# A hybrid HGRN2 and gated DeltaNet layer on one core: TensorE's order written down in halves of projections

## The chip, the cores and the metric

The kernel runs on one core of a Trainium2 chip, as one launch. The time is that of the device, in microseconds (us), for the whole program. "PE" is TensorE (matrix products), "DVE" VectorE, "ACT" ScalarE, "POOL" GpSimd, "SP" the engine whose queue issues nearly all DMAs here. PEld is TensorE's weight load, which runs beside its matmuls.

## The reference

One layer of a backbone over 2048 latent tokens and 256 context tokens, width 1024. A normalised and modulated input `h` goes through one projection of 9248 columns. Eight heads of kind A (HGRN2, a gated linear recurrence) and eight of kind B (gated DeltaNet, with a 3x3 depthwise convolution on q, k and v) scan the tokens forward and backward in chunks; both scans of the latents start from the state that the context leaves. The head outputs are normalised, gated, put through one output projection, added to the input and normalised again.

```python
def project(h, w_in, conv_w, lb, a_log, dt_bias, rows):
    y = jnp.einsum("bld,dn->bln", h, w_in)
    a_q, a_f_fwd, a_f_bwd, a_i, a_z, b_q, b_k, b_v, b_z, b_a, b_b = split_columns(y)
    ...
    qkv = jax.nn.silu(grid_conv(jnp.concatenate([b_q, b_k, b_v], axis=-1), conv_w, rows))

# group A, one chunk (hgrn2_scan)
        s_new = d_last[..., 0, :, None] * s + jnp.einsum("bhsk,bhsv->bhkv", k_dec, v_i)
        scores = jnp.einsum("bhtk,bhsk,bhtsk->bhts", q_i, k_i, dec)
        o = jnp.einsum("bhtk,bhkv->bhtv", q_dec, s) + jnp.einsum("bhts,bhsv->bhtv", scores, v_i)

# group B, one chunk (gdn_scan); u0 and w come from a triangular solve with the chunk's keys
        v_new = u0_i - jnp.einsum("bhck,bhkv->bhcv", w_i, s)
        s_new = d_last[..., None, None] * s + jnp.einsum("bhck,bhcv->bhkv", k_dec, v_new)
        o = jnp.einsum("bhtk,bhkv->bhtv", q_dec, s) + jnp.einsum("bhts,bhsv->bhtv", p_i, v_new)

# group_out, then the residual and the last norm
    y_a = jax.nn.silu(z_a) * head_norm(o_a, na_w)
    y_b = jax.nn.silu(z_b) * head_norm(o_b, nb_w)
    return jnp.concatenate([y_a, y_b], axis=-1) @ w_out
```

## The kernel before, in words

Tokens are worked in 9 groups of 256 (the context and eight of latents), each of two blocks of 128. Projections run in float16 with every operand split into a high and a low part: one step over 128 input channels is three matmuls (high by high, low by high, high by low), so a projection of one column block for one group is 8 x 3 = 24 matmuls (`proj_cm`, lines 401 to 407, into `pm`, and `proj_tm`, lines 392 to 398, into `pz`). The rest of TensorE's work is float32.

The program is a sequence of stages T (`all_heads`, line 1002): stage T projects group T mod 9 for A head p = T div 9, for the keys of B head p and for the values and queries of B head p-1. Beside the projections several dependent strands run, each a generator that yields between its steps:

- **chains** of a B head (`chain`, line 873), one per direction. For each block: p1 = k S into `pc` (L889), r = p1 scaled + v on DVE (L893), p2 = zb r (L894), `ud` and `u` copied out with a scale on ACT (L897, L900), p3 = k ud (L902) and P u (L911), and the new state S on DVE (L907). The next block's p1 needs that S.
- **the unit** of an A head and a group (`AHead.unit`, line 1198): a sigmoid of the q projection (`sg`, L1227), q on DVE (L1229), then scores at six levels m = 1 to 32; before each level DVE multiplies `QK` by a shifted copy `sk` that ACT makes (L1279 and L1267), and `level_products` (L1366, L1369) issues small matmuls into `sa`.
- **inverse levels** of a B head (`inverse_levels`, line 520), small matmuls into the bank `lv`; the weights of the next head (`prepare`, line 1079: `raw` is loaded by L371, squared on ACT in L373, split into `whi` and `wlo` on DVE); the convolution on DVE (`conv`, L690), keys, values, scores and the backward pass of A (`backward`, line 1388).

`interleave` (line 1125) steps these generators in turn, and with that the order in which the program names its instructions is set. The order in which each engine runs them is another one: a scheduler in the compiler, working from its own simulation of times, picks it for every engine and for SP's queue, by priorities (`high_priority(BURST)` and `issue_after` in `level_products` keep the small matmuls of a level together). So halves and pieces of a projection stand between the steps of strands as that simulation had it.

At the end (`Out`, line 1427) tiles of 128 tokens are normalised and transposed (`operands`, line 1497: two passes over 128x2048 on ACT, L1515 and L1517) and multiplied by the output weights (`products`, line 1527, L1535), two PSUM banks of 512 columns in alternation; the first three tiles are begun without the last head's columns.

Of the kernel before, what the change touches and what calls it, by code (L numbers as in the profile page):

```python
# [1 line left out]

# [6 lines left out]
F32 = mybir.dt.float32  # L9
# [352 lines left out]
def prep_w(K, cols, places):  # L362

    nc = K.nc
# [3 lines left out]
    for i, (col, (hi, lo)) in enumerate(zip(cols, places)):  # L368
# [5 lines left out]
        raws.append(raw)  # L374
    if K.lv is None:
# [13 lines left out]
    return [(hi, lo, un) for hi, lo in places]  # L389


def proj_tm(K, out, w, h):

    nc = K.nc
    for k in range(KC):
# [5 lines left out]
def proj_cm(K, out, w, h):  # L401

    nc = K.nc
    for k in range(KC):
# [67 lines left out]
def inverse_base(K, h, mt_d, im, ch0, nch):  # L472
# [22 lines left out]
    for m in range(1, 15):  # L495
# [6 lines left out]
        nc.vector.tensor_tensor(dst, dst, tv, op=ALU.add)  # L502
    ww = iv.tile([P, 2, 16, 16], F32, tag="w64", name="ww")[:nb]
# [13 lines left out]
    return w32  # L517


def inverse_levels(K, h, mt_d, w32a, first, ch0, nch, out):  # L520
# [32 lines left out]
    g, hh = prep(0, 16, w32[:, :, 0, :], w32[:, :, 1, :], 32)  # L553
    py = K.lv[:, :128].rearrange("p (c j) -> p c j", j=32)
# [4 lines left out]
    yield  # L559
# [8 lines left out]
    yield  # L568

    g, hh = prep(1, 32, w32[:, :, 0, :], w32[:, :, 1, :], 32)  # L570
    py = K.lv[:, :128].rearrange("p (c j) -> p c j", j=32)
# [5 lines left out]
    yield  # L577
    w64 = iv.tile([P, 2, 4, 2, 32], F32, tag="w64", name="w64")
    msk = K.off[32].bitcast(I32).unsqueeze(1).to_broadcast([P, nch, 2, 32])
    for st in range(2):  # L580
        nc.scalar.copy(w64[:, st, :nch], w32[:, :, st, :].unsqueeze(2).to_broadcast([P, nch, 2, 32]))
    for st in range(2):
# [10 lines left out]
        yield  # L593
# [3 lines left out]
    g, hh = prep(2, 64, w64v[:, 0, :nch], w64v[:, 1, :nch], 64)  # L597
    R64 = [slice(0, 64), slice(64, 128)]
# [6 lines left out]
    yield  # L605
# [12 lines left out]
    yield  # L618


class BHead:


    def __init__(self, K, h):
# [6 lines left out]
        self.S = [None, None]  # L631

    def project(self, gi, xs, hh):
        K, nc, w, pads = self.K, self.K.nc, self.w, self.pads
        R = GT // GRID_W
        for x in xs:
            if gi == 0 and x == "q":
                continue
            pm = K.pm.tile([P, GT], F32, tag="mm", name="pm")
            proj_cm(K, pm, w[x], hh)  # L640
# [3 lines left out]
            if gi == 0 or gi % 2:  # L644
                pads[x, u] = K.bp.tile([P, 2 * R + 2, GRID_W], F32, tag="pad" + x, name="pad")
            pad = pads[x, u]
            if gi == 0:
# [46 lines left out]

    def of_unit(self, u):
# [992 lines left out]
```

## Time and profile before

| | us |
|---|---|
| median of 3 runs | 3435.51 (3431.07 to 3439.38) |
| the profiled execution | 3429.3 |
| its span | 3427.6 |
| PE busy in it | 3135.9 (91%) |
| DVE, ACT, POOL busy | 2459.6 (72%), 1839.5 (54%), 1473.7 (43%) |
| mean granted TensorE clock | 0.972 of full speed |

All sums are made against one profiled execution: its time of 3429.3 us is its span of 3427.6 us and 1.7 us around it, and it stands 6.2 us under the median of the runs. Busy shares are means over stages with different limits; windows of the span and the waits within them tell more.

### The profile page before, as it was taken

The numbers are of one execution on the slowest core, as the hardware profiler recorded it, in microseconds if no ns is written. First come the engines' busy times: TensorE is split into PE (matmuls) and PEld (weight loads), VectorE is DVE, ScalarE is ACT, GpSimd is POOL, SyncE is SP. The second block draws the span as 40 slices with busy tenths as digits, with TensorE's granted clock in tenths as the row PEclk, the third lists the DMA queues.
The fourth block names the chain that finished last, engine by engine and source line by source line (L and its number), as shares of the span: only waits on it lengthen the run. The fifth ranks groups of instructions, "written<-read, shape, count | busy, mean of one in ns | idle before, by whom it ended". The sixth has DMA issues, their size and how long they took to land.

```text
span 3427.6 us, 95270 instructions
## 1 busy us (share of the span) xinstructions
PE 3135.9 (91%) x37768; PEld 2428.1 (71%) x37768; DVE 2459.6 (72%) x6531; ACT 1839.5 (54%) x4921; POOL 1473.7 (43%) x2534
## 2 busy tenths in 40 slices
PE   7878998999998999899999999999999899898998
PEld 3666777877787777777777777777777677755554
DVE  5867687778877876788678867886788677845332
ACT  5764555555655564556565555556455654644332
POOL 3525644465446443644464446444444243521010
PEclk9999999999999999999999999999999999999999
DMA  7744444454445444555455444544354544544331
GB/s 248 233 146 140 133 128 145 138 173 145 148 143 166 149 141 124 164 152 153 130 168 151 149 136 154 155 126 143 126 155 137 188 149 139 158 148 149 136 117 51
DMA packets 433475, 508.45 MB, mean 148 GB/s; under 512 B 110724, under 2 KB 336644, under 8 KB 420996
## 3 DMA queue, kind: packets, MB, share of 16 engines
q1 hardware_dynamic: 395908, 477.18, 44.4%
q10 hardware_dynamic: 37120, 25.18, 2.3%
q8 instruction: 297, 4.87, 0.6%
q14 instruction: 150, 1.23, 0.1%
HBM read 346.35 MB, written 155.88 MB: 147 GB/s over the span
## 4 chain that ended last, share of the span: by engine, by line
PE 39%; DVE 21%; DMA 16%; POOL 9%; ACT 8%; issue 5%; SPq 1%; ACTq 0%; DVEq 0%; POOLq 0%
PE po L1535 8%; DVE acc L690 5%; PE pm L405 4%; PE pm L407 4%; PE pm L406 4%; DMA raw<-in_w_in_dram 3%; DMA df<-dd 3%; DVE QK L1279 2%; POOL br L788 2%; POOL or L56 2%; DMA dc<-dc_d 2%; PE pz L398 2%; PE pz L396 2%; PE pz L397 1%; DMA y_d<-df 1%
## 5 line engine op out<-in xcount | busy, mean ns | idle before, releaser
L405 PE MATMUL pm<-h,whi 128*128 128x256 f16 x3256 | 900.3, 276 | 13.8 <-ACT pad L652 5.6
L407 PE MATMUL pm<-h,wlo 128*128 128x256 f16 x3256 | 898.9, 276 | 2.6 <-DVE wlo L388 2.6
L406 PE MATMUL pm<-h,whi 128*128 128x256 f16 x3256 | 899.3, 276 | 0.0
L690 DVE SCALAR_TENSOR_TENSOR acc<-pad,cw,acc 128x504 f32<-128x504 f32 (+1 forms) x768 | 585.6, 766 | 26.8 <-ACT acc L684 17.4
L396 PE MATMUL pz<-whi,h 128*128 128x384 f16 (+1 forms) x1152 | 362.0, 318 | 19.8 <-ACT pad L652 6.3
L406 PEld LDWEIGHTS <-whi 128*128 128x128 f16 x3328 | 330.9, 99 | 56.4 <-issue 14.4
L407 PEld LDWEIGHTS <-wlo 128*128 128x128 f16 x3328 | 330.7, 99 | 46.4 <-DVE wlo L388 3.9
L405 PEld LDWEIGHTS <-whi 128*128 128x128 f16 x3328 | 331.2, 100 | 44.9 <-ACT whi L385 2.0
L398 PE MATMUL pz<-whi,h 128*128 128x384 f16 (+1 forms) x1152 | 361.8, 318 | 0.0
L397 PE MATMUL pz<-wlo,h 128*128 128x384 f16 (+1 forms) x1152 | 361.4, 318 | 0.0
L1267 ACT COPY sk<-QK 128x512 f32<-128x512 f32 x384 | 242.4, 631 | 203.0 <-DVE QK L1279 150.6
L1279 DVE TENSOR_TENSOR QK<-QK,T 128x512 f32<-128x512 f32 x384 | 267.8, 697 | 49.0 <-ACT sk L1267 39.1
L1219 POOL TENSOR_SCALAR QK<-QK,omlb 128x256 f32<-128x256 f32 x144 | 154.9, 1083 | 210.4 <-ACT QK L1215 209.3
L788 POOL TENSOR_SCALAR br<-br,nbc 128x128 f32<-128x128 f32 x252 | 175.4, 712 | 81.5 <-DMA br<-row_d 55.3
L897 ACT ACTIVATE ud<-pc,rk 128x128 f32<-128x128 f32 x272 | 99.7, 367 | 171.8 <-PE pc L894 146.4
L920 POOL TENSOR_SCALAR_AFFINE_SELECT zb<-zb 128x256 f32<-128x256 f32 x144 | 68.4, 476 | 271.3 <-ACT zb L925 258.6
L1535 PEld LDWEIGHTS <-yh 128*128 128x128 f16 x1024 | 100.3, 98 | 110.2 <-ACT yh L1523 1.5
L542 POOL TENSOR_TENSOR g<-w,lm 128x128 f32<-128x128 f32 (+2 forms) x120 | 81.3, 677 | 208.6 <-DVE w L591 91.8
L397 PEld LDWEIGHTS <-h 128*128 128x128 f16 x1152 | 114.8, 100 | 78.6 <-issue 25.6
L398 PEld LDWEIGHTS <-h 128*128 128x128 f16 x1152 | 114.5, 99 | 61.5 <-issue 3.2
L396 PEld LDWEIGHTS <-h 128*128 128x128 f16 x1152 | 114.7, 100 | 56.7 <-issue 3.0
L920 POOL TENSOR_SCALAR_AFFINE_SELECT P<-vq 128x256 f32<-128x256 f32 x128 | 70.0, 548 | 181.1 <-PE pc L911 126.4
(368 smaller groups left out, 8074.9 us busy)
## 6 DMA issues: line engine op xcount, KB each, us to landing
h<-hT SPq DMA_DIRECT2D x72, 1024.0 KB
raw<-in_w_in_dram SPq DMA_DIRECT2D x72, 512.0 KB
kk<-kk_d SPq DMA_DIRECT2D x137, 256.0 KB
df<-dd SPq DMA_DIRECT2D x64, 512.0 KB
vq_d<-vq SPq DMA_DIRECT2D x56, 384.0 KB
vq<-vq_d SPq DMA_DIRECT2D x56, 384.0 KB
kk_d<-kk SPq DMA_DIRECT2D x72, 256.0 KB
br<-row_d SPq DMA_DIRECT2D x48, 384.0 KB
```

Source lines behind the costliest of these rows:

```text
L396: nc.tensor.matmul(out, lhsT=h(0, k), rhs=w[0][:, k, :], start=(k == 0), stop=False)
L397: nc.tensor.matmul(out, lhsT=h(0, k), rhs=w[1][:, k, :], start=False, stop=False)
L398: nc.tensor.matmul(out, lhsT=h(1, k), rhs=w[0][:, k, :], start=False, stop=(k == KC - 1))
L405: nc.tensor.matmul(out, lhsT=w[0][:, k, :], rhs=h(0, k), start=(k == 0), stop=False)
L406: nc.tensor.matmul(out, lhsT=w[0][:, k, :], rhs=h(1, k), start=False, stop=False)
L407: nc.tensor.matmul(out, lhsT=w[1][:, k, :], rhs=h(0, k), start=False, stop=(k == KC - 1))
L690: nc.vector.scalar_tensor_tensor(av[:, :, a:b], pad[:, 1 + dy:R + 1 + dy, a + dx:b + dx], wt(dy, dx), av[:, :, a:b], op0=ALU.mult, op1=ALU ...
L788: (nc.vector if h < 1 else nc.gpsimd).tensor_scalar(t[:, c, :], t[:, c, :], K.nbc[:, d, h, b + c:b + c + 1], None, op0=ALU.add)
L1219: nc.gpsimd.tensor_scalar(QK[:, 3 - 2 * d, :], QK[:, 3 - 2 * d, :], col(K.omlb, d), None, op0=ALU.mult)
L1267: nc.scalar.copy(view(sk, m, [[-m, 2], [2 * m, 2 * np_], [1, m]]), view(QK, m, [[2 * n - m, 2], [2 * m, 2 * np_], [1, m]]))
L1279: nc.vector.tensor_tensor(qk, qk, view(T, 0, [[nT + 1, 2], [2, 2 * np_], [0, m]]), op=ALU.mult)
L1535: nc.tensor.matmul(po[b], lhsT=l[:, j, :], rhs=r[k][:, b * 512:(b + 1) * 512], start=f, stop=e)
```

## The change

Every projection is issued in halves of 12 matmuls. After each half, a *slot*, each strand (a `Lane`) may do one step: first the chains of a B head, forward and backward, then the backward pass of A, the units, values, keys, decays, the weights and the inverse levels; small steps come in a second pass. A strand that yields n sleeps for n slots (the chains) or 2n slots (the others). The two sides of a chain's link are written two slots apart. At the end the program goes through its PE instructions after the set-up in the order in which they were named and makes each depend on the one before, so that this order is PE's order; no wait is added by that, since it is one engine's own order. The other engines and SP's queue are still ordered by the scheduler.

```diff
+HALVES = (range(KC // 2), range(KC // 2, KC))
+def in_halves(f, *args):
+    f(*args, HALVES[0])
+    yield
+    f(*args, HALVES[1])
...
             pm = K.pm.tile([P, GT], F32, tag="mm", name="pm")
-            proj_cm(K, pm, w[x], hh)
+            yield from in_halves(proj_cm, K, pm, w[x], hh)
...
+class Lane:
+    def run(self, slot, small):
+        while slot >= self.wake and self.small == small:
+            if self.until is not None:
+                if not self.until():
+                    return
+                self.until = None
...
+            x = next(self.now, END)
...
+                self.small = x == SMALL
+                self.wake = slot + self.unit * (1 if x is None or x == SMALL else x)
+class Slots:
+    def __init__(self, K):
+        self.cf, self.cb = Lane(K, CHAIN, 1), Lane(K, CHAIN, 1)
+        self.u0, self.u1, self.w, self.inv = (Lane(K, LEVEL) for _ in range(4))
+        self.ab, self.keys, self.v0, self.v1, self.dec = (Lane(K) for _ in range(5))
+    def go(self):
+        self.slot += 1
+        self.K.used = 0
+        for small in (False, True):
+            for x in self.lanes:
+                x.step(self.slot, small)
+    def fill(self, gen):
+        for _ in gen:
+            self.go()
...
             nc.vector.scalar_tensor_tensor(r, p1, col(K.neb), q["v"][:, c, :], op0=ALU.mult, op1=ALU.add)
+            yield 2
         nc.tensor.matmul(p2, lhsT=zb, rhs=r, start=True, stop=True)
...
             nc.scalar.activation(u, p2, AF.Copy, scale=q["rk"][:, 0, c:c + 1])
+        yield 2
         if not last:
             nc.tensor.matmul(p3, lhsT=q["kn"][:, c, :], rhs=ud, start=True, stop=True)
...
-        with K.tc.high_priority(BURST):
-            first = nc.tensor.matmul(ops[0][0], lhsT=ops[0][1], rhs=ops[0][2], start=True, stop=True)
-            with K.tc.issue_after(first.ins):
-                for out, k, q in ops[1:]:
-                    nc.tensor.matmul(out, lhsT=k, rhs=q, start=True, stop=True)
+        for out, k, q in ops:
+            nc.tensor.matmul(out, lhsT=k, rhs=q, start=True, stop=True)
...
+    prev = None
+    for i in traced[begun:]:
+        if i.engine == mybir.EngineType.PE:
+            if prev is not None:
+                tc.add_manual_dep(i, prev.name, mybir.DependencyInfo(
+                    mybir.DependencyClass.NoSync, mybir.DependencyReason.DATA), reason="slots")
+            prev = i
```

Around it: some buffers grow and others shrink to fit (key sets 2 to 3, `vq` 3 to 4, `dd` 10 to 20, the load buffers of `kk` in the chains now ahead of use, `jk` to 1); `h` of the next stage and the decay rows `dc` are loaded earlier in the program's text; in a step of a strand at most one tile of the pool `ps` is taken per slot (`turn`); A's backward pass adds its output block by block (64 adds of 128x256 become 128 of 128x128). At the end four tiles, not three, are begun early, with 12 of the 16 head columns instead of 14; one PSUM bank is filled after the other instead of both in alternation, from a pool of three; loads, transposes and products of the tiles take turns with the last head's chains by slots.

```diff
-W_ORDER = [*range(NH - 1), *range(NH, 2 * NH - 1), NH - 1, 2 * NH - 1]
-EARLY = 3
+W_ORDER = [*range(NH - 2), *range(NH, 2 * NH - 2), NH - 2, 2 * NH - 2, NH - 1, 2 * NH - 1]
+EARLY = 4
...
-        po = [ps.tile([P, 512], F32, tag=f"po{n}", name="po") for n in range(2)]
-        for n, k in enumerate(x for x in W_ORDER if x in ks):
+        for b in range(2):
+            ns = slice(b * 512, (b + 1) * 512)
+            po = ps.tile([P, 512], F32, tag="po", name="po")
+            for n, k in enumerate(wk):
...
+                    nc.tensor.matmul(po, lhsT=l[:, j, :], rhs=r[k][:, ns], start=f, stop=e)
+                if n % 2 and n < len(ks) - 1:
+                    yield
```

The work is the same: 42507 matmuls on PE before and after, 2539 operations on POOL; DVE's rows go from 6533 to 6602 and ACT's from 4395 to 4387.

**PE, inside a stage in the middle of the program.** The rows are PE's instructions in the order in which the built program has them; `pm` is a projection, `sa` scores of an A unit, `lv` an inverse level. Before, around one link of a chain (L889 is p1, L894 is p2):

```order
L749 MATMUL pk<-kk 128x128 x2
L889 MATMUL pc<-S,kk 128x128
L891 MATMUL pc<-S,vq 128x128
L1366 MATMUL sa<-QK 32x64
L1369 MATMUL sa<-QK 32x64 x7
L1369 MATMUL sa<-sk 32x32 x24
L894 MATMUL pc<-r,zb 128x128
L405 LDWEIGHTS whi
```

and in the changed program (L975 is p1, L981 is p2; the cut rows are the rest of the two halves of 12 projection matmuls each):

```order
L975 MATMUL pc<-S,kk 128x128
L977 MATMUL pc<-S,vq 128x128
L1599 MATMUL sa<-QK 32x64 x8
L1599 MATMUL sa<-sk 32x32 x24
L416 LDWEIGHTS whi
L416 MATMUL pm<-h,whi 128x256
...
L418 MATMUL pm<-h,wlo 128x256
L640 MATMUL lv<-g,y 64x64 x8
L416 LDWEIGHTS whi
...
L418 MATMUL pm<-h,wlo 128x256
L981 MATMUL pc<-r,zb 128x128
```

Before, only other strands' small matmuls stand between the two ends of this link; now two halves do.

**PE, at the end of the program.** Now `po` is the output projection. Before, with both banks in alternation (the cut rows are more of the same, 15 output matmuls in all between the two ends):

```order
L889 MATMUL pc<-S,kk 128x128
L891 MATMUL pc<-S,vq 128x128
L1535 LDWEIGHTS yh
L1535 MATMUL po<-whi,yh 128x512
L1522 MATMUL pt<-ident,y 128x128 x8
...
L894 MATMUL pc<-r,zb 128x128
```

and in the changed program (12 output matmuls, one bank):

```order
L975 MATMUL pc<-S,kk 128x128
L977 MATMUL pc<-S,vq 128x128
L1807 LDWEIGHTS yh
L1807 MATMUL po<-whi,yh 128x512
L1807 LDWEIGHTS yh
L1807 MATMUL po<-wlo,yh 128x512
...
L981 MATMUL pc<-r,zb 128x128
```

There the link's cover went from a varying number of matmuls and transposes to a fixed 12 matmuls.

## Rows read from the trace of the kernel before

**Rows 1.** Head of the profile page: each engine's busy us, share, instructions.

```profile
PE 3135.9 (91%) x37768; PEld 2428.1 (71%) x37768; DVE 2459.6 (72%) x6531; ACT 1839.5 (54%) x4921; POOL 1473.7 (43%) x2534
```

**Rows 2.** Windows of start, middle and end; the first line names the columns.

```profile
core 0: us, PE busy (x) PEld busy (x) DVE busy (x) ACT busy (x) POOL busy (x), PEclk, DMA share, GB/s
0.00:350.00 350.00, 283.43 (x2986) 202.44 (x2986) 243.65 (x649) 210.17 (x426) 148.98 (x266) 0.94 0.59 192
350.00:2950.00 2600.00, 2410.12 (x32169) 1972.35 (x32168) 1999.12 (x5410) 1441.27 (x4102) 1236.04 (x2103) 0.98 0.48 147
2950.00:3428.00 478.00, 442.32 (x2615) 253.28 (x2615) 216.77 (x472) 188.06 (x394) 88.69 (x165) 0.96 0.37 126
```

**Rows 3.** Three windows of 100 us from the middle, same columns.

```profile
450.00:550.00 100.00, 87.18 (x1108) 72.48 (x1109) 82.98 (x227) 56.37 (x143) 40.72 (x59) 0.95 0.49 141
1050.00:1150.00 100.00, 89.09 (x1226) 71.82 (x1224) 81.20 (x229) 54.36 (x161) 54.83 (x96) 1.00 0.57 175
1650.00:1750.00 100.00, 96.95 (x1258) 80.88 (x1255) 69.15 (x181) 51.48 (x150) 49.26 (x85) 1.00 0.45 144
```

**Rows 4.** PE's waits, 350 to 2950: us in total, times, longest us.

```profile
PE pc L894 <- DVE r L893: 16.7, 21, 2.3
...
PE lv L380 <- ACT wlo L373: 12.0, 11, 3.4
...
PE pk L834 <- DMA kk<-kk_d: 6.7, 5, 3.4
...
PE po L1395 <- DMA df<-dd: 6.5, 6, 1.9
...
PE sa L1366 <- DVE QK L1279: 2.9, 3, 1.2
```

**Rows 5.** Waits of ACT for a load, and of SP's queue, same stretch.

```profile
ACT wlo L373 <- DMA raw<-in_w_in_dram: 87.5, 34, 6.0
...
SPq L371 <- DVE wlo L388: 136.6, 40, 11.7
```

**Rows 6.** Timeline of PE: start, duration, line, operation; three kinds of projection.

```profile
1505.83 0.27 PE L406 MATMUL pm<-h,whi 128*128 128x256 f16 x1
1505.94 0.27 PE L407 MATMUL pm<-h,wlo 128*128 128x256 f16 x1
...
1525.15 0.32 PE L396 MATMUL pz<-whi,h 128*128 128x384 f16 x1 [0.80 <-DVE q L1229]
1525.32 0.32 PE L397 MATMUL pz<-wlo,h 128*128 128x384 f16 x1
...
3329.78 0.59 PE L1535 MATMUL po<-whi,yh 128*128 128x512 f16 x2
3330.21 0.59 PE L1535 MATMUL po<-wlo,yh 128*128 128x512 f16 x2
```

**Rows 7.** Timeline of one chain link: p1 on PE, and r on DVE.

```profile
1515.32 0.39 PE L889 MATMUL pc<-S,kk 128*128 128x128 f32 x2
...
1515.97 0.35 DVE L893 SCALAR_TENSOR_TENSOR r<-pc,neb,vq 128x128 f32<-128x128 f32 x1 [0.55 <-PE pc L891]
```

**Rows 8.** Timeline of one A unit: its sigmoid, and DVE's last level multiplication.

```profile
1523.21 0.47 ACT L1227 ACTIVATE sg<-pm,wv 128x256 f32<-128x256 f32 x1
...
1536.61 0.68 DVE L1279 TENSOR_TENSOR QK<-QK,T 128x512 f32<-128x512 f32 x1
```

**Rows 9.** Groups by line: count, busy us, mean ns of one, idle before.

```profile
L1267 ACT COPY sk<-QK 128x512 f32<-128x512 f32 x384 | 242.4, 631 | 203.0 <-DVE QK L1279 150.6 <-DVE QK L1233 29.9 <-PE sa L1369 5.4
L1279 DVE TENSOR_TENSOR QK<-QK,T 128x512 f32<-128x512 f32 x384 | 267.8, 697 | 49.0 <-ACT sk L1267 39.1 <-PE sa L1369 8.4
...
L979 DVE TENSOR_TENSOR o<-o,pc 128x128 f32<-128x128 f32 x128 | 35.7, 279 | 1.3
...
L1517 ACT ACTIVATE y<-y,ws 128x2048 f32<-128x2048 f32 (+2 forms) x19 | 32.8, 1727 | 3.8 <-DVE wu L68 3.8
L1515 ACT ACTIVATE yl<-y 128x2048 f16<-128x2048 f32 (+2 forms) x19 | 31.2, 1641 | 63.0 <-DMA y<-y_d 46.3 <-PE po L1535 16.8
```

More of the change, by code (lines that the diff above doesn't have):

```diff
@@ L1 @@
+from collections import deque
 from contextlib import ExitStack, nullcontext
+from itertools import chain, islice
 import concourse.bass as bass
@@ L362, in prep_w, with prep_steps @@
 def prep_w(K, cols, places):
+    out = []
+    for _ in prep_steps(K, cols, places, out):
+        pass
+    return out
+def prep_steps(K, cols, places, out):
     nc = K.nc
@@ L374, in prep_w @@
         raws.append(raw)
+    yield 3
     if K.lv is None:
@@ L900, in chain @@
             nc.scalar.activation(u, p2, AF.Copy, scale=q["rk"][:, 0, c:c + 1])
+        yield 2
         if not last:
             nc.tensor.matmul(p3, lhsT=q["kn"][:, c, :], rhs=ud, start=True, stop=True)
+        if out is not None:
+            nc.tensor.matmul(p1, lhsT=q[f"P{d}"][:, c, :], rhs=u, start=True, stop=True)
+        if not last:
             sn = K.ck.tile([P, P], F32, tag=f"S{d}", name="S", bufs=2 + d)
@@ L956, in group @@
         q = self.q[gi]
[L957 to L963 removed]
+        ahead = d == 0 or first or self.load_back(gi)
         self.masked(gi, d)
@@ L1002, in all_heads @@
 def all_heads(K, A, B):
     np_ = max([*A, *(i + 1 for i in B)]) + 2
+    L = K.slots
+    ahead = None
     for T in range(N, N * np_):
@@ L1072, in prepare_early, with into, together @@
         _, at = columns(K)
-        a.w["f"], a.w["b"] = prep_w(K, [COL["af"] + P * a.h, COL["ab"] + P * a.h], at[:2])
-        yield
-        a.w["q"], = prep_w(K, [COL["aq"] + P * a.h], at[2:])
+        yield from together([(2, into(K, a, "fb", [COL["af"] + P * a.h, COL["ab"] + P * a.h], at[:2])),
+                             (1, into(K, a, "q", [COL["aq"] + P * a.h], at[2:]))])
+def into(K, x, names, cols, places):
+    out = []
+    yield from prep_steps(K, cols, places, out)
+    for n, w in zip(names, out):
+        x.w[n] = w
+def together(gens):
+    on, gens = [], deque(gens)
+    while on or gens:
+        for x in list(on):
+            x[1] -= 1
+            if x[1] <= 0:
+                n = next(x[0], END)
+                if n is END:
+                    on.remove(x)
+                else:
+                    x[1] = n or 1
+        if gens and sum(x[2] for x in on) + gens[0][0] <= 2:
+            m, g = gens.popleft()
+            n = next(g, END)
+            if n is not END:
+                on.append([g, n or 1, m])
         yield
@@ L1475, in begin, with all_weights @@
         nc.sync.dma_start(self.gt, K.gt_d.rearrange("a b -> (a b)").unsqueeze(0).broadcast_to([P, D]))
-        self.fw = oc.tile([P, D], F32, name="fw")
+        self.fw = self.oc.tile([P, D], F32, name="fw")
         nc.sync.dma_start(self.fw, self.a["final_norm_w"].unsqueeze(0).broadcast_to([P, D]))
+    def all_weights(self, part):
+        if part == 0:
+            yield from self.weights(0, 3)
+            return
+        self.K.done.discard("Z")
+        for n, x in enumerate("YXZ"):
+            while x not in self.K.done:
+                yield
+            yield from self.weights(3 * n + 3, 3 * n + 6)
@@ new lines, in tiles @@
+        load(1)
+        for _ in range(6):
+            yield
+        for _ in self.transposes(*made[0]):
+            yield
+        for n in range(len(todo)):
+            m = made[n][1]
+            work = self.products(*made[n])
+            nxt, age = None, 0
+            for j, _ in enumerate(work):
+                load(n + 1)
+                if len(made) > n + 1:
+                    age += 1
+                    if age > 6 and (j >= m // 2 or m < 8) and j % 2:
+                        nxt = nxt or self.transposes(*made[n + 1])
+                        next(nxt, None)
```

662 lines of the change are left out of this document (401 added, 261 removed).

## The prediction

> **What bounds the kernel now.** I read the head of the page first: PE is busy for 3135.9 of 3427.6 us, DVE for 2459.6 [rows 1]. PE has no work it could lose here, since the change keeps its 42507 matmuls; what can be won is its idle time, 3427.6 - 3135.9 = 291.7 us, and the part of its work that runs at the lower clock.
>
> Next the windows, to see where the idle time lies [rows 2]. Start (0 to 350): 350 - 283.4 = 66.6 us. Middle (350 to 2950): 2600 - 2410.1 = 189.9 us. End (2950 to 3428): 478 - 442.3 = 35.7 us. The granted clock is 0.98 in the middle. The two levels are 1.2 and 2.4 GHz, so 2 x (1 - 0.98) x 2600 = 104 us of the middle ran at the lower one, in which 52 us of full-speed work was done: the clock costs about 52 us there.
>
> Single windows of the middle differ [rows 3]: 1650 to 1750 has PE at 96.95 of 100 us, 1050 to 1150 at 89.09, 450 to 550 at 87.18. So the kernel can already run a stretch of this very work with 3% idle, when the order happens to suit it.
>
> Then the waits of PE in the middle [rows 4]. The reader is to see that no wait dominates: the largest group, p2 for r, is 16.7 us in 21 waits of at most 2.3 us. Most are links of a strand whose answer comes back from DVE, ACT or POOL a microsecond or two after PE has run out of other things. Few are loads: `kk` 6.7, `df` 6.5, and 12.0 for ACT's pass over `raw`, which itself waits for its load.
>
> **How long a link is, and what covers it.** In one link p1 begins at 1515.32 and r ends at 1515.97 + 0.35 = 1516.32, so 1.0 us [rows 7]. The longest wait of this link, 2.3 us, comes on top of what cover it had [rows 4]. Before, of 500 such links (p1 to p2, p2 to p3) in the stretch with projections, counted over the built order, 77 have fewer than 8 projection matmuls between their ends and 122 fewer than 12. In the changed order each of 485 has 24. A 256-column projection matmul takes 1505.94 - 1505.83 = 0.11 us, a 384-column one 1525.32 - 1525.15 = 0.17 [rows 6], so a link has 2.6 us or 4 us of projection, and the strands' own matmuls on top. Counted by all the work between a wait of PE and the PE instruction it hangs on, waits with less than 3 us of work in front fall from 613 to 99 in the middle.
>
> **The change, term by term** (own time 3429.3, span 3427.6).
>
> *Middle, idle.* Lower end: nothing won, if every wait returns in other clothes (0). Upper end: only the three load rows stay, 12.0 + 6.7 + 6.5 = 25.2 us [rows 4], so -165. Between them stands the best window, 3.05% idle, which over 2600 us would leave 79 us, or -111 [rows 3]. The new order gives each link more than that window gave all of its own, so I take a value between window and upper end: 60 us left, **-130**.
>
> *Middle, clock.* 0 to -52. The two windows at 96.95 and at 89.09 were both granted 1.00, the one at 87.18 only 0.95 [rows 3]; so less idling can bring the clock back, but the share of idle time alone doesn't set it. I take less than half, **-20**.
>
> *Start.* The set-up isn't touched; its last part runs without chains. **0**, within 10 either way.
>
> *End.* Idle is only 35.7 us [rows 2], so at most -20 is in reach. A link there now has 12 matmuls of 512 columns; three groups of two run in 0.43 us each, 0.22 us one [rows 6], so 2.6 us. ACT's two passes over a whole tile take 1.64 and 1.73 us, 64 us together for 38 of them [rows 9], which is 13% of 478 us. A `u` that meets one waits half of it, 0.85 us. Counted in the order, 77 waits at the end have less than 3 us of work in front: 77 x 0.13 x 0.85 = 9, **+10**, at worst +40 if most meet a pass.
>
> *What costs nothing.* A's 64 adds over a whole group become 128 over a block, like those of 279 ns [rows 9]: 128 x 0.279 = 36 us of DVE at most, less the 64 that go, hidden as long as DVE isn't the bound. It had 1999 us of work in the middle [rows 2]; at the new length of about 2450 us that is 82%, a share that it reached in the window 450 to 550 [rows 3]. Loads: `h` is named a stage earlier, into the same two buffers, so on SP it stands ahead of some `raw`, `kk` and `df` loads. The list of PE's waits has none for `h`; if its 1 MB pushes `kk` or `df` back, the rows of 6.7 and 6.5 us are what grows. SP itself stood 136.6 us before `raw` loads because the buffer wasn't free yet [rows 5]; those still have two buffers, and everything behind them in SP's queue still waits. I leave that in the 60 us. The PE dependencies wait for nothing, since they only fix one engine's own order.
>
> Sum: -130 - 20 + 0 + 10 = -140, a span of 3287.6 and, with the 1.7 us around it, a time of 3289; I say **3290**. The runs' median is 6.2 us above the profiled execution, inside the rounding of these terms.
>
> **Rivals.**
>
> *Buffers, not order (chance 0.11).* If PE waits because a tile isn't free, writing the order down renames the waits. A chain keeps one `pc` tile per direction, `ps` has two. For it: the pools of the chains didn't grow. Against: the waits listed are for results (r, u, `wlo`), and none repeats as one gap; 16.7 of 190 us is the largest [rows 4]. Then the middle keeps its idle time and perhaps a tenth goes: 3429.3 - 15 = 3414, and half of this case is no change. The Trainium skill ("Perfetto Trace Analysis", section Optimization Strategy) says that the same gap, repeating on the engine that should be saturated, can mean too few buffers for the next tile; by that rule an order alone would win nothing, and this trace shows no such single gap.
>
> *Other queues keep their order (0.10).* Only PE's is fixed. ACT stood 87.5 us before `raw` loads [rows 5], with chain copies behind it in its queue. Before, the scheduler could put PE's waits where it thought ACT late. If all of it now passes to PE: 3429.3 - 140 + 87.5 = 3377.
>
> *Head of line on PE, the slower side (0.11).* Now PE can't go around a late strand: what is named first blocks all behind it. The tightest strand is the A unit. Its path from `sg` to the last level's multiplication took 1523.21 to 1536.61 + 0.68, 14.1 us [rows 8]; the bare work of six levels is 6 x (0.631 + 0.697) = 8.0 us [rows 9] plus 0.47 for `sg`. In the new order 48 + 48 projection matmuls stand between the q projection and its last such products: 48 x 0.17 + 48 x 0.11 = 13.4 us, and some 6 us of strands' matmuls in those 8 slots: the order has 9984 projection matmuls of 256 columns and 3072 of 384, 9984 x 0.11 + 3072 x 0.17 = 1620 us in 1088 halves, nearly all in the middle, and the other 790 of its 2410.1 us are 0.73 for each half. So 19 against 14.1, a margin of 5 us. If DVE, at 82%, makes every unit miss by 4 us all the same, 64 units cost 256: 3429.3 - 140 + 256 = 3545. It decides from a mean lateness of 140 / 64 = 2.2 us on. Against it: PE's wait of `sa` for `QK` is only 2.9 us now [rows 4]. The Trainium skill ("PSUM — Partial Sum Buffer", section Engine vs sequencer instructions) states that matmuls start and complete in program order; it is the rule that speaks against writing an order down, and how late a strand may come it doesn't say.
>
> **How the numbers follow.** Forecast 0.68, the rivals 0.11, 0.10, 0.11. Range: the bounds of the forecast alone are -165 - 52 - 20 and 0 - 0 + 40, which no one run will join; I take 3200 (the upper ends of idle and clock together, with a little given back) to 3395, which covers the forecast with weaker idle gains and the second rival, and leaves the first and the third out, 0.2 together. Faster by over 0.2% (7 us, about what a measurement can tell): 0.68 + 0.10 + half of the first rival = 0.84; within: 0.05; slower: 0.11.
>
> **What would show it.** Right: in the middle PE's idle share is 2 to 3% in nearly all windows of 100 us, the wait of p2 for r is under 5 us, what is left are loads, and the clock there is 0.99. Wrong by buffers: the waits of PE name the reader of an older tile. Wrong by queues: ACT or SP waits for loads have grown and PE waits for `u`, `ud` or `wlo`. Wrong by head of line: `sa` waiting for `QK` has grown from 2.9 us to a hundred. At the end: idle near 45 us and `u` behind L1515's pass.

## The result, and the profile after

The changed kernel takes 3510.24 us in the median (3509.05 to 3521.75), beside 3434.91 for the kernel before in the same runs: a ratio of 1.0226, with a 95% interval of 1.0201 to 1.0251. It is slower by 2.3%; forecast were 3290 us and a gain, in a range up to 3395. The profiled execution of the changed kernel is the longest of its four, with a span of 3520.0 us, 92.4 more than the one before. The head of its page answers to [rows 1]:

```profile
span 3520.0 us, 95277 instructions
...
PE 3114.7 (88%) x37768; PEld 2428.3 (69%) x37768; DVE 2471.4 (70%) x6600; ACT 1845.0 (52%) x4914; POOL 1490.4 (42%) x2534
```

PE is busy for 21 us less, and idle for 405.3 us instead of 291.7. To see where, the two traces are cut where the same work is done: after the first 1734 of the 13872 projection matmuls, and at the last of them. Windows of the kernel before, by these marks (columns as in [rows 2]):

```profile
0.00:384.00 384.00, 314.10 (x3362) 227.61 (x3363) 257.01 (x691) 228.34 (x479) 166.20 (x298) 0.94 0.57 185
384.00:2978.30 2594.30, 2405.53 (x32074) 1967.91 (x32071) 2010.20 (x5420) 1441.92 (x4102) 1237.54 (x2098) 0.98 0.48 147
2978.30:3428.00 449.70, 416.25 (x2336) 232.55 (x2334) 192.34 (x421) 169.25 (x342) 69.96 (x140) 0.95 0.36 126
```

and of the changed kernel:

```profile
0.00:436.30 436.30, 326.34 (x3631) 238.62 (x3632) 277.36 (x731) 232.31 (x494) 180.40 (x322) 0.88 0.53 172
436.30:3037.50 2601.20, 2357.67 (x31582) 1948.35 (x31580) 1993.31 (x5413) 1429.97 (x4040) 1237.41 (x2054) 0.96 0.47 145
3037.50:3520.00 482.50, 430.66 (x2560) 241.36 (x2558) 200.74 (x458) 182.75 (x381) 72.58 (x160) 0.95 0.35 118
```

The start loses 52 us, the middle 7, the end 33. In the middle, for which 150 us of gain were forecast, two things cancel. PE is busy for 48 us less, although its clock is lower (0.96 for 0.98: by these rounded values about 104 us more at 1.2 GHz, which cost about 52), so its work there became about 100 us cheaper. A part of that is work that moved: 492 matmuls fewer (31582 for 32074) stand in the middle, and about as many more at the start and the end. But PE is idle for 243.5 us instead of 188.8. Its waits, between 350 and 2950 us as in [rows 4]:

```profile
PE pc L975 <- DVE op L1090: 79.4, 43, 4.5
PE pc L975 <- DVE o L1093: 30.6, 24, 2.8
PE sa L1599 <- ACT sk L1484: 26.9, 12, 9.1
PE lv L391 <- ACT wlo L383: 22.3, 12, 2.9
PE lv L584 <- DMA mt<-mt_d: 21.4, 2, 16.0
PE pc L981 <- DVE r L979: 15.7, 13, 2.1
PE pc L990 <- ACT u L987: 11.8, 9, 2.9
```

The many small waits of before are mostly gone. In their place stands one: p1 of a chain's next block (L975) waits for the output steps `op` or `o` of the block before, 110 us in 67 waits. Before they made 6.6 us together, in these rows of the same view (the last of them is for the rivals below):

```profile
PE pc L889 <- DVE o L979: 3.9, 5, 1.1
...
PE pc L889 <- DVE op L976: 2.7, 4, 1.0
...
PE sa L1366 <- ACT sk L1267: 0.5, 1, 0.5
```

The output steps read the bank `pc`; a direction has one such bank, and p1 writes it. The longest of these waits on the timeline, all engines, with what stands ahead of `op`:

```profile
1298.88 0.39 PE L993 MATMUL pc<-u,P 128*128 128x128 f32 x2
...
1302.27 0.33 DVE L999 SCALAR_TENSOR_TENSOR S<-S,el,pc 128x128 f32<-128x128 f32 x1
...
1302.63 1.06 ACT L383 ACTIVATE wlo<-raw 128x1024 f16<-128x1024 f32 x1 [1.67 <-DMA raw<-in_w_in_dram]
...
1304.03 1.40 DVE L399 SCALAR_TENSOR_TENSOR wlo<-raw,ws,whi 128x512 f16<-128x512 f32 x2
1304.04 0.25 ACT L1089 COPY op<-pc 128x128 f32<-128x128 f32 x1
...
1306.27 0.33 DVE L1090 SCALAR_TENSOR_TENSOR op<-pc,neb,op 128x128 f32<-128x128 f32 x1
...
1306.65 0.49 PE L975 MATMUL pc<-S,kk 128*128 128x128 f32 x2 [4.55 <-DVE op L1090]
```

P u is done at 1299.3. S is made only three microseconds later, when DVE comes to it; the copy of `op` stands on ACT behind a pass over raw weights that itself waited 1.67 us for its load; its second half stands on DVE behind two passes of `wlo` and three other operations. The link takes 7.4 us from P u's end to p1, for work of about 1 us, and its 24 projection matmuls had ended by 1302.1.

### The profile page after: what moved, and what is told of

The parts are those of the page before. It is cut to its first block, busy times and chain, and to the rows that moved or that the text cites. A ratio compares the mean times of both kernels' runs of the same rounds, so it can differ in the third digit from the quotient of the medians.

```text
span 3520.0 us, 95277 instructions
## 1 busy us (share of the span) xinstructions
PE 3114.7 (88%) x37768; PEld 2428.3 (69%) x37768; DVE 2471.4 (70%) x6600; ACT 1845.0 (52%) x4914; POOL 1490.4 (42%) x2534
## 4 chain that ended last, share of the span: by engine, by line
PE 35%; DVE 21%; DMA 14%; issue 11%; ACT 10%; POOL 8%; SPq 1%; ACTq 0%; POOLq 0%; DVEq 0%
DVE acc L724 5%; PE pm L416 5%; PE pm L417 4%; PE pm L418 4%; DMA df<-dd 3%; PE po L1807 3%; DVE QK L1494 2%; PE pz L407 2%; PE pz L408 2%; PE pz L409 2%; ACT sk L1484 2%; POOL br L850 2%; DMA br<-row_d 2%; DMA raw<-in_w_in_dram 1%; POOL or L58 1%
## 5 line engine op out<-in xcount | busy, mean ns | idle before, releaser
L416 PE MATMUL pm<-h,whi 128*128 128x256 f16 x3256 | 918.0, 282 | 5.3 <-DVE g L1334 4.8
L417 PE MATMUL pm<-h,whi 128*128 128x256 f16 x3256 | 915.1, 281 | 0.0
L418 PE MATMUL pm<-h,wlo 128*128 128x256 f16 x3256 | 914.1, 281 | 0.0
L724 DVE SCALAR_TENSOR_TENSOR acc<-pad,cw,acc 128x504 f32<-128x504 f32 (+1 forms) x768 | 565.4, 755 | 16.9 <-ACT acc L718 11.5
L416 PEld LDWEIGHTS <-whi 128*128 128x128 f16 x3328 | 339.5, 102 | 52.0 <-DVE g L1334 1.0
L417 PEld LDWEIGHTS <-whi 128*128 128x128 f16 x3328 | 335.4, 101 | 48.7 <-issue 5.5
L1494 DVE TENSOR_TENSOR QK<-QK,T 128x512 f32<-128x512 f32 x384 | 276.8, 721 | 90.8 <-ACT sk L1484 68.4
L1418 POOL TENSOR_SCALAR QK<-QK,omlb 128x256 f32<-128x256 f32 x144 | 182.1, 1273 | 232.5 <-ACT QK L1414 219.1
L975 PE MATMUL pc<-S,kk 128*128 128x128 f32 x544 | 120.0, 304 | 123.5 <-DVE op L1090 81.3
L975 PEld LDWEIGHTS pc<-S,kk 128*128 128x128 f32 x544 | 89.2, 198 | 154.6 <-DVE op L1090 95.1
L830 ACT ACTIVATE sg<-acc 128x256 f32<-128x256 f32 x208 | 79.5, 412 | 160.7 <-DVE acc L724 133.5
L409 PEld LDWEIGHTS <-h 128*128 128x128 f16 x1152 | 114.6, 99 | 68.5 <-issue 3.2
```

The costliest lines, as they stand in the source:

```text
L409: nc.tensor.matmul(out, lhsT=h(1, k), rhs=w[0][:, k, :], start=False, stop=(k == KC - 1))
L724: nc.vector.scalar_tensor_tensor(av[:, :, a:b], pad[:, 1 + dy:R + 1 + dy, a + dx:b + dx], wt(dy, dx), av[:, :, a:b], op0=ALU.mult, op1=ALU ...
L975: nc.tensor.matmul(p1, lhsT=q["kT"][:, c, :], rhs=s, start=True, stop=True)
L1494: nc.vector.tensor_tensor(qk, qk, view(T, 0, [[nT + 1, 2], [2, 2 * np_], [0, m]]), op=ALU.mult)
```

## The experiments

Each ratio is that of the named kernel to the kernel before, measured on the same chip; medians of different calls aren't compared. The traces come from several chips, on which the kernel before itself took between 3420.84 and 3434.91 us in the median, so ten microseconds between two traces are no finding. The theories: **A**, the order fixed on PE makes it stand at the head of its line; **B**, the rest of the new text costs the time; and from the first results on **C**, the queues of DVE and ACT, each served in its own order, answer late and pace the middle as much as PE does. P is the premise of the prediction, that PE's idle time is free to be won.

**The order alone.** e1_free leaves out the dependencies between PE's instructions; e11_free_burst also keeps the small matmuls of a level together again.

```diff
-    for i in traced[begun:]:
+    for i in []:
```

> The changed kernel without the dependencies that fix PE's order; the scheduler picks PE's order again from the same text, pools and halves. Theory A (the fixed order makes PE stand at the head of its line for answers that DVE and ACT give late: 80 and 33 us of p1 waiting for the output steps op and o): the time comes back to the kernel before or below, 3390 to 3450 us, and p1's wait for op and o in the middle falls from 113 us to under 25. Theory B (the new text, pools and buffers cost the time whatever the order): it stays above 3480.

Measured: 1.0638 (1.0612 to 1.0663). Theory A as it stood falls: without the fixed order the same text is far slower, not back at the kernel before. p1's wait for `op` and `o` in the middle did fall, to 12 us, and bought nothing. The page:

```profile
span 3653.5 us, 95298 instructions
...
PE 3325.8 (91%) x37768; PEld 2528.8 (69%) x37768; DVE 2458.8 (67%) x6600; ACT 1853.7 (51%) x4919; POOL 1542.3 (42%) x2534
```

PE is idle for 78 us less than with the order fixed (327.7 for 405.3), but busy for 211 us more, with the same instructions: the time is lost inside its work. The inverse levels show it. Windows over the whole span of tile `lv` alone, changed kernel:

```profile
0.00:4000.00 4000.00, 174.81 (x8174) 139.41 (x8174) 96.38 (x332) 39.49 (x152) 0.95 0.41 127
```

and e1_free:

```profile
0.00:4000.00 4000.00, 293.87 (x8174) 199.31 (x8174) 97.09 (x332) 39.27 (x152) 0.95 0.41 127
```

The first number behind the length is PE's busy time: the same 8174 small matmuls take 174.8 us where they stand together (in 332 pieces without another tile's matmul between) and 293.9 where they are strewn (842 pieces), at the same mean clock. This is the time in which at least one of them runs, whatever else runs beside it. Counted by what each adds behind the end of the matmul before it, the two traces give 151 and 234 us, so 83 of the 211 us are theirs.

```diff
+        with K.tc.high_priority(3000):
+            first = nc.tensor.matmul(ops[0][0], lhsT=ops[0][1], rhs=ops[0][2], start=True, stop=True)
+            with K.tc.issue_after(first.ins):
+                for out, k, q in ops[1:]:
+                    nc.tensor.matmul(out, lhsT=k, rhs=q, start=True, stop=True)
```

> The changed kernel with PE's order left to the scheduler and the small matmuls of a level of scores kept together again as in the kernel before. It divides the change: if the first free run lost its 220 us over the kernel before only by scattering these small matmuls among the projections (sa took 130 us there, 100 before), this run comes to a ratio of 0.995 to 1.015 and PE's fixed order costs the rest of the changed kernel's 1.0226; if the text's priorities, halves and buffers cost it otherwise, it stays over 1.035 and the fixed order wins back what the text loses.

Measured: 1.0377 (1.0349 to 1.0405). So the change has two halves of opposite sign: the text with its priorities, halves and buffers costs 3.8%, and the fixed order, against this free one, wins 1.5% of it back. Which part of the text costs the 3.8% wasn't taken apart further. What the fixed order wins is not what was forecast:

```profile
span 3556.5 us, 95377 instructions
...
PE 3223.6 (91%) x37768; PEld 2468.9 (69%) x37768; DVE 2460.3 (69%) x6600; ACT 1846.1 (52%) x4917; POOL 1536.4 (43%) x2534
```

Beside this run, the changed kernel has PE busy for 109 us less (3114.7) and idle for 72 us more (405.3 for 332.9). p1's waits for `op` and `o` are 19 us in the middle here and 110 there. The fixed order makes PE's work cheaper and its idle time longer.

**The links.** e2_gap3 gives the link that waits most a third half, e13_links1 takes one of two from the links to p2 and p3.

```diff
             if j < GC - 1:
-                yield 2
+                yield 3
```

> The changed kernel with one more slot between P u of a chain's block and p1 of the next (three halves instead of two, 36 matmuls instead of 24). Theory A with the bank pc as its place (p1 must write the bank that op still reads): the 113 us of p1 in the middle fall under 40 and the time by 70 to 110 us, to 3400 to 3440. If the lateness only moves to the next thing in line, or the chain becomes too long for its stage: 3480 to 3530.

Measured: 1.0350 (1.0329 to 1.0372), slower still. PE's waits in the same stretch:

```profile
PE lv L391 <- ACT wlo L383: 52.3, 11, 8.4
PE sa L1599 <- ACT sk L1484: 41.6, 16, 7.3
PE pc L981 <- DVE r L979: 37.7, 35, 1.9
...
PE pc L975 <- DVE o L1093: 20.1, 13, 2.5
```

The wait at the bank went, from 110 us to 30 (`op` is 9.8 us, in a row further down), and others rose in its place: for `wlo`, `sk` and `r`, none of which the edit touches. Middle and end, by the marks from above:

```profile
436.70:3036.50 2599.80, 2325.24 (x31470) 1930.07 (x31469) 1985.48 (x5394) 1432.36 (x4026) 1254.39 (x2048) 0.96 0.47 144
3036.50:3547.00 510.50, 442.98 (x2672) 248.25 (x2670) 208.52 (x477) 186.23 (x393) 74.80 (x163) 0.92 0.35 115
```

The middle is as long as in the changed kernel (2599.8 for 2601.2). What this trace loses lies behind the last projection, 510.5 us for 482.5: 318 `pc` and 416 `lv` matmuls are left for it, where 302 and 320 were, since the chains have become longer. So more distance at one link takes its wait away and not the lateness behind it, and it puts the chains' end off.

```diff
-            yield 2
+            yield 1
         nc.tensor.matmul(p2, lhsT=zb, rhs=r, start=True, stop=True)
...
-        yield 2
+        yield 1
         if not last:
             nc.tensor.matmul(p3, lhsT=q["kn"][:, c, :], rhs=ud, start=True, stop=True)
```

> The changed kernel with one half (12 projection matmuls, 1.3 us) instead of two between p1 and p2 and between p2 and p3. The prediction's theory of cover: links of 1 us and more come back as waits, r and u in the middle grow from 27 us to over 100, and the time by 60 to 150 us, ratio over 1.04. Theory C (the answers' place in DVE's and ACT's queues decides, not the count of matmuls between): r and u grow, p1's wait for op and o shrinks, and the time stays within 30 us of the changed kernel, ratio 1.014 to 1.031.

Measured: 1.0427 (1.0407 to 1.0447). Here the prediction's count of matmuls between the ends holds, and theory C's range does not:

```profile
PE pc L981 <- DVE r L979: 114.4, 72, 5.7
...
PE pc L975 <- DVE op L1090: 18.7, 16, 5.3
```

p2 waits for r 114 us instead of 16. Two halves are needed at that link, and three at the link to the next p1 don't pay. The distance matters as long as it is shorter than the answer, and the answer is often longer than the bare link of 1 us: even behind two halves r came late 13 times.

**Start and end.** e3_start_free fixes the order from the third stage on, e8_late_pin from the second head's stages, e4_end_free up to the last stage with projections. All three change where the loop over PE's instructions begins or ends, e8_late_pin for instance:

```diff
-    for i in traced[begun:]:
+    for i in traced[marks[2 * N]:]:
```

> PE's order is fixed only from the third stage of projections on. If the first stages lose their 50 us (the 867 x 2 first projections end at 436 us instead of 384) because PE is held in order behind weights and keys that arrive late: 3455 to 3470. If the loss there comes from the text's order of loads and weights: no change, 3500 to 3520.

Measured: 1.0234 (1.0213 to 1.0256), no change. By its trace the first sixteenth of the projections was done at 194 us (188 in the kernel before, 253 in the changed one), and the second sixteenth at 433 (436 in the changed one). Where the order was fixed again, the time was given back.

> PE's order is fixed only from the second head's stages on. With the order free throughout, the sixteenth of the projections that ends at 436 us ended at 386, as in the kernel before at 384. If the start's 50 us are head of line on weights, keys and the inverse's load: 3450 to 3470. If the loss only moves behind the start, as with two free stages: 3500 to 3520.

Measured: 1.0178 (1.0152 to 1.0203), between the two outcomes that were expected. With the whole first head's stages free the mark that lay at 436 us lies at 388.6, with the clock at 0.94 again:

```profile
0.00:388.60 388.60, 323.98 (x3465) 233.45 (x3466) 267.19 (x711) 231.50 (x489) 177.49 (x304) 0.94 0.57 187
```

So the start's loss comes from the fixed order: PE stands at the head of its line. Its waits up to 436 us in the changed kernel say for what:

```profile
PE lv L584 <- DMA mt<-mt_d: 20.6, 2, 16.0
PE pq L391 <- ACT wlo L383: 16.2, 2, 14.7
PE pk L807 <- DVE MT L810: 15.2, 3, 10.9
```

The longest single waits, of 11 to 16 us, are for a load (`mt`), for weights (`wlo`) and for the tile `MT` that DVE makes; the order lets nothing pass them. How much of these 48 us the whole program gains is less sure than their place: the ratio moved by 0.5%, some 16 us.

> PE's order is fixed only up to the last stage with projections; the end is the scheduler's. If the end's loss of 33 us (from the last sixteenth of the projections to the end 483 us instead of 449) is head of line: 3475 to 3485. If it comes from the end's new layout (one bank after the other, four early tiles): 3500 to 3520.

Measured: 1.0201 (1.0180 to 1.0223). The end took 472.5 us by its trace, 10 less; the ratio doesn't tell that from nothing. So by this trace most of the end's loss is not head of line. What is left of it is mostly work: after the last projection 302 `pc` matmuls still stand to be run, 230 in the kernel before, and 320 `lv` where 96 stood, so the chains come later out of the slots.

**The bank's last reader.** e7_op_dve moves the copy of `op` from ACT to DVE, behind S on the same queue.

```diff
-                nc.scalar.copy(o[:, c, :], o2)
+                nc.vector.tensor_copy(o[:, c, :], o2)
```

> The first output step op of a chain's block is copied out by DVE instead of ACT, so that S, op and its second half stand on one queue; ACT loses 128 copies of 0.27 us, DVE gains them (some 36 us). If the hop over ACT, behind its passes over raw weights, is what keeps the bank: p1's wait for op falls from 80 us to about the 33 us of o, and the time by 20 to 50, to 3460 to 3490. Theory C: DVE is the pace, so the time stays or rises, 3505 to 3550.

Measured: 1.0180 (1.0159 to 1.0201), some 16 us by the ratio. DVE got 128 operations more and the kernel became rather faster than slower, against theory C's range, so DVE's load is not all. But the row of `op` fell from 79.4 to 58.7 us only, and a third row of p1 came up:

```profile
PE pc L975 <- DVE op L1090: 58.7, 34, 4.9
PE pc L975 <- DVE o L1093: 33.2, 27, 3.2
...
PE pc L975 <- DVE wq L66: 15.2, 7, 3.2
```

Together p1 still waits 107 us for DVE, where it waited 111 (with 1.0 us in a third row there). So the hop over ACT is not what decides how long the bank is kept, and where the 16 us were won isn't shown.

**Whose pace.** Work is taken from DVE or from PE, first in the changed kernel, then in the kernel before.

```diff
-                    if dy == 0 and dx == 0:
+                    if (dy == 0) == (dx == 0):
```

> The changed kernel with the four corner taps of the 3x3 convolution left out: 384 of 768 DVE additions of 0.755 us go, about 285 us of DVE's 2471, and nothing of PE's work. Theory C (PE's fixed order runs ahead of its feeders, and DVE's and ACT's queues, served in order, set the pace of the middle, which took 2594 to 2601 us in the kernels before, changed, with three slots, with a free start and a free end): the time falls by over 80 us, to under 3430. Theory A2 (only the place of the steps in PE's order counts): it falls by less than 30, to 3480 or above.

Measured: 0.9970 (0.9952 to 0.9989), 2.6% under the changed kernel, some 88 us, inside theory C's range. The middle is where it was won, with PE idle for 181.8 us instead of 243.5:

```profile
425.70:2921.10 2495.40, 2313.57 (x31582) 1928.60 (x31581) 1775.92 (x5063) 1435.88 (x4040) 1160.42 (x2050) 0.97 0.49 151
```

The rows of p1 are still 98 us together, so it was mostly won elsewhere. The run doesn't take from DVE alone: POOL's same 2534 operations took 1406.6 us by its page, 1490.4 in the changed kernel.

```diff
         nc.tensor.matmul(out, lhsT=w[0][:, k, :], rhs=h(0, k), start=(k == 0), stop=False)
-        nc.tensor.matmul(out, lhsT=w[0][:, k, :], rhs=h(1, k), start=False, stop=False)
-        nc.tensor.matmul(out, lhsT=w[1][:, k, :], rhs=h(0, k), start=False, stop=(k == KC - 1))
+        nc.tensor.matmul(out, lhsT=w[0][:, k, :], rhs=h(1, k), start=False, stop=(k == KC - 1))
```

> The changed kernel with the third product of each projection step left out (high by low of one operand): a third of the projection matmuls, about 560 us of PE at full clock by 4480 x 0.11 to 0.17, and nothing of DVE's. Halves have 8 matmuls then, so the slots are a third shorter. If PE is the pace of the middle: the time falls by over 400 us, to under 3110. Theory C: most of it becomes waiting and the time falls by less than 250, to over 3260.

Measured: 0.9645 (0.9625 to 0.9666), 5.8% or 200 us under the changed kernel, inside theory C's bound: about a third of what was taken from PE. With the work went cover, since a half has 8 matmuls here, and clock: the mean granted one was 0.910, 0.947 in the changed kernel.

> The kernel before with the four corner taps of the convolution left out: 285 us less for DVE, PE's work as it was. Theory C (the middle is paced by PE and by the queues of DVE and ACT together, in the kernel before too, so that its 190 us of idle PE were never free to win by an order): 60 to 120 us less than before, ratio 0.965 to 0.983. Theory P, the prediction's premise (before, DVE at 82% has room and PE's idle is a matter of order alone): less than 30 us, ratio over 0.991.

Measured: 0.9923 (0.9902 to 0.9944), 26 us: in this point P's range holds and theory C's doesn't. DVE's load alone is not what paces the kernel before.

> The kernel before with the third product of each projection step left out, about 560 us of PE. Theory P: over 400 us less, ratio under 0.885. Theory C: 150 to 280 us less, ratio 0.92 to 0.955, and the idle time of PE grows by the rest.

Measured: 0.9671 (0.9647 to 0.9695), 113 us. That is less than either theory gave:

```profile
span 3307.2 us, 86013 instructions
...
PE 2774.0 (84%) x33144; PEld 2100.5 (64%) x33144; DVE 2431.0 (74%) x6531; ACT 1833.7 (55%) x4922; POOL 1546.3 (47%) x2534
```

A third of the projections is gone, and the kernel loses 3.3%. PE's busy time fell by 362 us, not by the estimated 560, because its clock fell (0.908 of full speed, 0.972 before), and most of the rest turned into waiting for many strands:

```profile
PE pc L892 <- DVE r L891: 32.4, 35, 5.1
PE pc L909 <- DVE S L905: 32.3, 37, 3.9
PE po L1393 <- DMA df<-dd: 29.9, 16, 3.6
PE pc L900 <- ACT u L898: 25.1, 33, 2.3
```

Premise P falls with this as far as it said that PE's work alone sets the time. The run does not show that no order could have won PE's idle time: the matmuls that are gone also covered links, and a theory of cover expects waits like that for r, 32.4 us here and 16.7 before.

**Do the gains add up?** e12_three puts the order's free start, its free end and e7's copy together; e14_three_ff adds a step of the A unit on ACT instead of DVE, e15_before_ff does that to the kernel before; e16_three_early puts the old division of the early output tiles into e12.

> The three single gains over the changed kernel in one (order free in the first head's stages, free at the end, op copied out by DVE). If they add up: 1.0226 - 0.0048 - 0.0025 - 0.0046 = 1.011. If the middle's pace takes them back: over 1.016. Neither theory lets it beat the kernel before.

Measured: 1.0105 (1.0089 to 1.0120): they add up. By the same marks as above its start, middle and end are

```profile
0.00:394.70 394.70, 325.13 (x3465) 234.11 (x3466) 269.04 (x718) 232.18 (x488) 179.45 (x306) 0.94 0.57 185
394.70:2978.10 2583.40, 2335.01 (x31751) 1934.42 (x31749) 2013.83 (x5550) 1412.22 (x3934) 1272.17 (x2071) 0.97 0.47 147
2978.10:3453.00 474.90, 435.76 (x2556) 247.18 (x2554) 200.17 (x462) 178.02 (x370) 69.21 (x159) 0.95 0.36 120
```

Its middle is 11 us shorter than that of the kernel before, which is no more than chips differ, and PE is idle in it for 248.4 us, as in the changed kernel: none of the three won that idle time. The end is 25 us longer.

```diff
-            nc.vector.tensor_scalar(FF[:, r, :], FF[:, x, :], col(K.omlb, d), col(K.lb, d), op0=ALU.mult, op1=ALU.add)
+            nc.scalar.activation(FF[:, r, :], FF[:, x, :], AF.Identity, scale=col(K.omlb, d), bias=col(K.lb, d))
```

> The three mends (ratio 1.0105) and the three scalings FF of each A unit on ACT instead of DVE: 216 operations of 0.42 us, some 90 us, leave DVE's queue, and ACT, which made their input, goes on without a hop. Theory C: lateness of answers falls, 15 to 35 us, ratio 1.000 to 1.006. If ACT's queue with its waits for raw weights is as much the pace as DVE's: no gain, 1.008 to 1.016.

Measured: 1.0067 (1.0052 to 1.0082), 0.4% under e12, a little short of theory C's range.

> The kernel before with FF on ACT in the same way. Leaving out 285 us of DVE gave it 26 us, so 90 us should give some 8 and the hop saved as much again: ratio 0.994 to 0.999. If a step less in the A unit's path counts more than DVE's load: under 0.994.

Measured: 1.0074 (1.0059 to 1.0089): the same edit makes the kernel before slower, against both outcomes that were expected. Here the scheduler lays PE's queue anew around the edit as well; whether that is the reason isn't shown.

> The three mends with the old division of the early output tiles: three tiles begun early with 14 of 16 head columns instead of four with 12. The end still took 475 us there against 449 in the kernel before. If the division is why: 10 to 25 us less, ratio 1.003 to 1.008. If it is the one bank after the other and the turns with the chains: within 5 us, 1.009 to 1.012.

Measured: 1.0108 (1.0091 to 1.0125), no change: the division of the early tiles is not why the end is longer. No version that does the whole work beat the kernel before; e14 came nearest.

Theory C's ranges held in e5 and e6, failed in e7, e9, e10 and e13, and e14 missed narrowly. That answers come late to a fixed order, and that this costs time, is shown by the waits and by e5; that DVE's and ACT's queues pace the middle as much as PE does is not.

## Why the prediction was wrong

*"What can be won is its idle time", 291.7 us.* This is the step that failed, and with it the term *Middle, idle*: two halves of projections were to cover every link, so that an order written down for PE would fill its gaps. The runs show the other sign. With the same text PE is idle for 327.7 us where the scheduler orders it (e1_free; 332.9 in e11_free_burst), and for 405.3 where the order is fixed; in the kernel before it was 291.7. Part of this may come from PE's cheaper work, which covers less. But the dependencies, which by the prediction wait for nothing, also hold PE at answers that are late: p1 waits 110 us for `op` and `o` with the order fixed, 12 and 19 us without. Behind this, PE's 91% were read as the bound; e10 gives back only 113 us of some 560 taken from PE, so its busy share says little of what less work for PE is worth. The Trainium skill ("Perfetto Trace Analysis", sections Identifying Performance Opportunities and Identifying the Most-Contended Engine) says that one generally improves the most-contended engine, the one with the highest occupancy, and adds that matmul busy is not a good measure of how close PE is to its roofline. By occupancy this is PE, at 91%, so the first half of the rule leads where the prediction went. This case agrees with its second half: in e10, with a third of the projections gone, PE is still busy for 84% of the span.

*Middle, idle: -130.* Measured +55. The links that were counted (p1 to p2, p2 to p3) weren't won: r stayed at 15.7 us of wait, where under 5 were the sign of being right and 16.7 was the wait before. Distance does count there, since e13 shows 114 us with half of it. But the step took a link's need to be its bare 1.0 us [rows 7], read from one link, and it put no price on another link, P u to the next p1, which passes through S, ACT and DVE and holds a bank. There the answer took 7.4 us in the row shown, and p1 waited 110 us in all. The upper end, "only the three load rows stay", did not think of that row at all.

*Middle, clock: -20.* The sign was wrong: 0.96 for 0.98, which costs about 52 us more. In the start it fell as well (0.88 for 0.94).

*Not in the sum:* PE was said to have no work that it could lose. Its work in the middle became about 100 us cheaper at full clock, in part because matmuls moved to the start and the end, in part because steps of a strand now stand together (over the whole program `lv` and `pc` keep PE busy for 208.6 and 507.0 us before, 174.8 and 463.7 now, with what other tiles run beside them). This is the gain that the change did bring, and the clock took half of it back.

*Start: 0 within 10.* Measured +52, of which e8 shows 48 to come from the fixed order. The prediction priced it by the set-up, and overlooked that PE can stand there for the first head's weights, keys and inverse.

*End: +10, at worst +40.* Measured +33, inside the bounds by luck, for other reasons: 18 us longer idle and 14 us more work, since the chains have more left when the projections end.

*What costs nothing.* DVE's share in the middle is 77% (1993 of 2601), below the 82% that was called harmless, and it was 77% before as well (2010 of 2594). So the share doesn't tell what DVE's work costs: 285 us less of it gave 26 us in the kernel before (e9) and 88 us with PE's order fixed (e5). In the row shown, `op` waited for its place in two queues.

*The rivals.* Head of line on PE had the right sign and the wrong place: `sa` for `QK`, priced at up to 256 us, did not grow (2.9 us before, 2.1 now). The unit is late at its other operand, `sa` for `sk`, with 26.9 us where it was 0.5, a tenth of that price. Where PE does stand is the chain's p1. Buffers: the bank `pc` is what p1 waits for, 67 times, and the wait names the reader of an older tile, the sign given for this rival; here the rule on consistent bubbles of the Trainium skill ("Perfetto Trace Analysis", section Optimization Strategy) has a row to go with it. But e2 took that wait away and the middle became no shorter, so the buffer is where the lateness shows and not where it comes from. A second bank for each direction wasn't tried. The second rival, the order of the other queues, fits the row shown best: ACT's wait for `raw` stayed (93.3 us, 87.5 in [rows 5]) and now reaches PE through `op` and `wlo`. But e7 left p1's wait as it was without ACT in its path, so ACT's part is argued and not shown. The size given, 3377 us, was wrong, since it still counted the whole gain of 140.

What stays open: which part of the new text costs its 3.8% without the fixed order, and with that why the changed kernel is slower than the one before; and which single queue, if any, sets the pace of about 2600 us in the middle. ACT's, POOL's and the loads' share in it wasn't tried.

## What to carry to other kernels

Before pricing idle time of the busiest engine as winnable, take work away from that engine on the chip: here a third of its projections was worth 3%, with the cover and the clock that went with them. Compare the same text with the order free and fixed: here the fixed order made PE's work cheaper and its idle time longer. When an order is written down for one engine, count every link, those over two queues and those that hold a buffer included, and give each the time its answer takes in a full queue, from rows, not the time of the bare work. Try leaving the order free where the strands are not in a steady state: here a free start won about 0.5%, a free end no more than the noise.

## What the runs showed of the hardware

Small matmuls cost PE more when they are strewn among others: 8174 `lv` matmuls kept PE busy for 174.8 us in 332 pieces and for 293.9 us in 842. Of this difference 83 us are time added to PE's, and the rest overlaps other matmuls. Less work for PE went with a lower granted clock: 0.908 with a third of the projections left out and PE busy for 84% of the span, against 0.972 at 91%, so that some 560 us of work at full clock (an estimate from 0.11 and 0.17 us for a projection matmul, [rows 6]) freed only 362 us of PE.
